# A hybrid recurrent decoder layer: ScalarE makes the convolution's first product from PSUM and the scaled diagonal of branch D, in place of GpSimd

## The chip, the core and the metric

The kernel runs on one core of one Trainium2 chip: TensorE for matrix products, VectorE, ScalarE and GpSimd for the rest, SyncE as the queue of the DMAs. The metric is the device time of one execution in microseconds, smaller is better. Each engine works through its own queue in order and waits on semaphores for the others. TensorE writes to PSUM; VectorE and ScalarE can read PSUM, GpSimd works on SBUF here.

## The reference

One inference step of one layer: layer norm, an input projection of 1024 to 3340 columns, four branches, an output projection, and a second layer norm. 2048 prompt tokens with 16 meta tokens ahead of them, and 8 sample sequences of 4 tokens, go through it.

```python
def _causal_conv(x, buf, w, b):          # branches A and C: 4 taps per channel, with bias
    xx = jnp.concatenate([buf, x], axis=1)
    y = lax.conv_general_dilated(xx, w[:, None, :], (1,), 'VALID', ..., feature_group_count=c)
    return y + b, xx[:, -3:]
...
xbc = jax.nn.silu(_causal_conv(xbc, ...))                  # A: Mamba-2 SSD
qkv = jax.nn.silu(_causal_conv(qkv, ...))                  # C: gated DeltaNet, q and k L2-normalised
...
def step(s, inp):                                          # D: HGRN2, per chunk
    qi, ki, vi, gi = inp                                   # gi: cumulated log decays
    dec = jnp.exp(jnp.where(i >= j, gi[:, :, None] - gi[:, None], -jnp.inf))
    a = jnp.einsum('bihk,bjhk,bijhk->bijh', qi, ki, dec)   # score matrix
    o = jnp.einsum('bijh,bjhv->bihv', a, vi) + jnp.einsum('bihk,bhkv->bihv', qi * jnp.exp(gi), s)
```

Branch B is a diagonal complex state space model (S5). All branch outputs are normalised per head or gated, concatenated, and projected back.

## The kernel before

All tensors are float32; products of the projections are made of high and low parts, three matrix products for each of 8 blocks of the 1024 input channels, so 24 for one block of results. The tokens are taken in two halves (`BLK`): half 0 in blocks of 304, 384 and 384 tokens, half 1 in two blocks of 512. For each half, phase 1a normalises and transposes the input, and phase 1b (`proj`) goes through column tiles of 128 channels; ten of these are convolution tiles (`conv_tile`: q, k and v of branch C, x, B and C of branch A). After both halves come the chunks of branches C and A, the gates, and the output projection.

TensorE runs in the order in which the program is written out. Chains that depend on each other ("jobs", such as `d_group` for branch D, `l2n`, `c_pre`, `b_main`) are generators that yield an estimate in microseconds; they are woven between the products of the projections by the sum of TensorE's costs so far. The order of most instructions on the other engines and of the DMAs on SyncE is set when the program is built, by a simulated timeline. The estimates in the yields stay the same in the change.

A projection's 24 products of a block go to a PSUM tile `pj`, of which there are two; when the block is done, `use` consumes it. In a convolution tile, `use` copies the block to `raw` (line 635, ScalarE; in the first block of half 0, where histories of the samples lie between the tokens, lines 626 to 632), with the last three columns of the block before in front of it. GpSimd then makes the product with the fourth tap and the bias into `cv` (line 639), VectorE adds the other three taps (line 641), and ScalarE takes the SiLU (lines 647 to 652). `raw` has three buffers, `cv` two. There are 50 such blocks: ten tiles by five blocks.

Branch D (`d_group`) takes two chunks of 128 tokens at a time (chunk 0 with 48 tokens alone): nine groups. The score matrix `AT` (128 x 8 x 128: token j, chunk and head, token i) starts as a diagonal, made from the column sums `sd` of q*k (line 1604, VectorE) and the identity by one wide product on GpSimd (line 1606). Then come levels s = 1, 2, 4 ... 64. In a level below 32, TensorE multiplies keys and queries, VectorE extends the queries `Q` (line 1666), GpSimd the keys `kS` (line 1667), and a predicated copy on VectorE (line 1670) puts the level's products into `AT`. The next level's products need lines 1666 and 1667 of this one. Line 580 makes the low parts of the next column tile's weights on GpSimd after ScalarE's rounding (line 579). Lines 1142 and 1151 are GpSimd's steps of branch B, lines 787 and 789 VectorE's steps of a triangular inverse.

Of the kernel before, what the change touches and what calls it, by code (L numbers as in the profile page):

```python
# [70 lines left out]
class Pinned:  # L71
    """An engine whose instructions don't move ahead of earlier ones."""
# [8 lines left out]
class Chain:  # L81
    """An engine whose instructions issued through here stay in the order in which they are written."""
# [14 lines left out]
class Kern:  # L97
# [12 lines left out]
    # The tensor engine runs in the order in which the kernel is written out. Dependent chains  # L110
    # are generators ("jobs") that yield the time until their next step can start; they are
    # woven between the matrix products of the projections.
# [64 lines left out]
    # ---------------------------------------------------------------- constants  # L177
    def consts(self, cp):
        nc, V, S, G = self.nc, self.V, self.S, self.G
        a = self.a  # L180
        self.ident = cp.tile([128, 128], F32, name="ident")
        make_identity(nc, self.ident)
        self.ones = cp.tile([128, 128], F32, name="ones")
        V.memset(self.ones, 1.0)
        self.triu = cp.tile([128, 128], F32, name="triu")
        G.affine_select(out=self.triu, in_=self.ones, compare_op=ALU.is_ge, fill=0.0,
                        base=0, pattern=[[1, 128]], channel_multiplier=-1)
        self.negm = cp.tile([128, 128], F32, name="negm")
        V.tensor_scalar(self.negm, self.triu, -1.0, 1e30, op0=ADD, op1=MUL)
        self.hsel = cp.tile([128, 2], F32, name="hsel")  # L190
        V.memset(self.hsel, 0.0)
        V.memset(self.hsel[0:64, 0:1], 1.0)
        V.memset(self.hsel[64:128, 1:2], 1.0)
        # sums the two parts of 32 channels of a head
        self.sel32 = cp.tile([128, 2, 32], F32, name="sel32")
        iv = self.ident.rearrange("p (a i) -> p a i", a=4)
        for h in range(2):
            V.tensor_tensor(self.sel32[:, h], iv[:, 2 * h], iv[:, 2 * h + 1], ADD)
        e9 = self.cst.rearrange("p a b -> p (a b)")[:NSEG, 0:48]
        V.memset(e9, 1.0)  # L200
        G.affine_select(out=e9, in_=e9, compare_op=ALU.is_ge, fill=0.0,
                        base=-12, pattern=[[1, 48]], channel_multiplier=-4)
        G.affine_select(out=e9, in_=e9, compare_op=ALU.is_ge, fill=0.0,
                        base=15, pattern=[[-1, 48]], channel_multiplier=4)
        V.memset(e9[0:1, 0:16], 1.0)
        p = self.pt()
        self.mm(p[:48, 0:48], e9, e9)
        self.segones = cp.tile([48, 48], F32, name="segones")
        V.tensor_copy(self.segones, p[:48, 0:48])
        p = self.pt()  # L210
        self.tr(p[:48, 0:NSEG], e9)
        self.segmask = cp.tile([48, NSEG], F32, name="segmask")
        V.tensor_copy(self.segmask, p[:48, 0:NSEG])
        self.triu_t = cp.tile([48, 48], F32, name="triu_t")
        V.tensor_tensor(self.triu_t, self.triu[:48, :48], self.segones, MUL)
        self.negm_t = cp.tile([48, 48], F32, name="negm_t")
        V.tensor_scalar(self.negm_t, self.triu_t, -1.0, 1e30, op0=ADD, op1=MUL)

    # ---------------------------------------------------------------- phase 1
    def small_loads(self, cp):  # L220
        """Job: small parameters, and the conv histories of the sample sequences channel-major."""
        a, V = self.a, self.Vp
        yield 8.2
        # channel-major small parameters, through one transpose
# [29 lines left out]
        # HGRN2 lower bound: softmax over the single layer, cumulative sum minus the first entry  # L254
# [70 lines left out]
    def phase1a(self, half, xp):  # L325
        """Layer norm and transposition of the input, and the products whose results are wanted token-major.
        The first yield comes before anything that needs the space of xh, xl or the weight ring."""
# [46 lines left out]
        def weights(i, parts):  # L374
            """u | i, dt, a, b: high and low parts."""
# [23 lines left out]
        else:  # L399
            # the first tile waits for as little as possible: one row comes by DMA, the other through the tensor engine  # L400
# [81 lines left out]
    def gates_in(self, half, sp):  # L482
# [3 lines left out]
        o = 1 - half          # chunk 0, the tail, is the first of half 0  # L486
# [14 lines left out]
        # softplus = max(x, 0) + log1p(e), log1p(e) = 2 atanh(e / (2 + e))  # L501
# [20 lines left out]
        # beta = sigmoid  # L522
# [7 lines left out]
        # inclusive cumulative sums inside each chunk, and the chunk totals  # L530
# [20 lines left out]
        if o:  # L551
            # decays of the tail segments, on every partition
# [8 lines left out]
        # rows: 0-7 cumulative logs, 8-15 their exponentials  # L561
# [21 lines left out]
    def proj(self, tiles):  # L583
        """tiles: (first column, per-block consumer, hook at the start); the next tile's weights are made ready first."""
# [20 lines left out]
    def conv_tile(self, i, c0, dst=None, nrm=None):  # L605
        """Causal conv and SiLU of one 128-channel tile, block by block.
        The first block is laid out as 8 x (3 history, 4 sample) | 3 zeros | meta | prompt."""
# [14 lines left out]
        def use(t0, n, p):  # L622
# [16 lines left out]
            G.tensor_scalar(cv[:, 0:m], raw[:, 3:3 + m], w[3], b, op0=MUL, op1=ADD)  # L639
# [22 lines left out]
    def l2n(self, st, dst, scale, nd, need, key):  # L662
        """Job: L2 normalisation over the channels of a head, for the blocks of a conv tile."""
# [54 lines left out]
    def decay(self, pool, tag, t, rows0, nh, bufs=None):  # L718
        """exp(acum_i - acum_j) for i >= j of one segment, 0 elsewhere, as [j, head, i]."""
# [10 lines left out]
    def c_pre(self, p):  # L730
        """Job: decayed K K^T and Q K^T of two heads, transposed."""
# [29 lines left out]
    def base_inv(self):  # L761
        """Inverses of the diagonal blocks of I + M, one block to a partition: 32 x 32 in the
        prompt chunks, 16 x 16 in chunk 0, whose segments don't cross multiples of 16."""
# [34 lines left out]
    def stream_out(self, c0, outs, mark=None):  # L798
        """outs: list of (function of (dst, psum)), dram destination)."""
# [53 lines left out]
    def conv_states(self):  # L853
        """Job: the conv states that go out."""
# [11 lines left out]
    # ---------------------------------------------------------------- branch B  # L866
    def exp_acc(self, pool, dst, x):
        """dst = exp(x) in float32 accuracy, for small tiles."""
# [20 lines left out]
    def b_setup(self, bp, tp):  # L889
# [56 lines left out]
        # powers of lambda, d = 0..8  # L946
# [21 lines left out]
        # rotating frame over chunks of 8  # L968
# [38 lines left out]
        # input matrices  # L1007
# [28 lines left out]
        # output matrices: Xc = (Cr | -Ci), Yc = (-Ci | -Cr)  # L1036
# [25 lines left out]
        # W1 = in-state matrices [(j q), (re n | im n)]  # L1062
# [15 lines left out]
        # block Toeplitz  # L1078
# [17 lines left out]
        # signed multipliers for single steps: h' = re * h + im_s * swap(h)  # L1096
# [187 lines left out]
    # ---------------------------------------------------------------- chunks  # L1284
# [85 lines left out]
    def c_inv(self, t0):  # L1370
        """Of two chunks: the inverse of I + M from the inverses of its 32 x 32 diagonal blocks,
        transposed; the values and the keys decayed to the end of the chunk, token-major."""
# [71 lines left out]
    def c_chunk(self, t, ep, y6):  # L1444
# [10 lines left out]
        # v_new = beta T (v - e^gc k S)  # L1455
# [33 lines left out]
    def c_head(self, ep, y6):  # L1489
        """Chunk 0: its nine segments start from their own states."""  # L1490
# [11 lines left out]
        # decay-scaled queries and keys  # L1502
# [50 lines left out]
    def tail_state(self, S9, kd, vflat, cdf, stage):  # L1553
        """S9[(h d), seg, pair, cols] <- decay * S9 + k^T v over each segment's tokens."""
# [21 lines left out]
    def d_group(self, t0c, nch, sfx):  # L1576
        """HGRN2 for nch chunks of 128 tokens (or chunk 0, 48 tokens); yields between its levels."""
# [22 lines left out]
        for c in range(nch):  # L1600
            for g in range(2):
# [4 lines left out]
        G.tensor_tensor(AT[:n, :4 * nch, :n], self.ident[:n, None, :n].to_broadcast([n, 4 * nch, n]),  # L1606
                        sd[:n, :nch].rearrange("p c h -> p (c h)")[:, :, None].to_broadcast([n, 4 * nch, n]), MUL)
# [6 lines left out]
        while s < lim:  # L1614
            # in the tail, blocks beyond 4 exist only in the 16 prompt tokens
# [9 lines left out]
            if s >= 32:  # L1625
                # few blocks: the keys block-diagonal by head, of the left halves alone
# [35 lines left out]
            # extend prefixes of the right halves, suffixes of the left halves, and the block products  # L1662
# [76 lines left out]
    def rms(self, t):  # L1739
        """Per-head RMS norms of a chunk."""  # L1740
# [5 lines left out]
        # The vector engine's transposes bring 32 channels at a time into the free dimension; small  # L1746
        # products add the two parts of a head and put the tokens onto their partitions.
# [28 lines left out]
    def gate(self, t):  # L1776
        """The norms and gates go onto a chunk."""
# [14 lines left out]
    def mix_chunk(self, t):  # L1792
        """The gated mix of a chunk, channel-major, rows A C D B, as high and low parts."""
# [11 lines left out]
    def out_setup(self, op, op2):  # L1805
        """Job: the output weights as high and low parts."""
# [19 lines left out]
    def out_chunk(self, t):  # L1826
# [24 lines left out]
        if last:  # L1851
            # the vector engine takes one part of the columns, the scalar engine and GpSimd the other
# [43 lines left out]
    def right_jobs(self):  # L1896
        """Branches B and D, in the space that phase 1 leaves, as their inputs come."""
# [66 lines left out]
    # ---------------------------------------------------------------- all  # L1964
# [89 lines left out]
    def head(self, ct):  # L2054
        """Chunk 0 of branches C and A."""
# [94 lines left out]
```

## Time and profile before

| | us |
|---|---|
| median of 3 runs | 1452.7 |
| lowest and highest run | 1446.28, 1456.98 |
| the profiled execution, first to last instruction (its span) | 1448.2 |
| TensorE busy (its weight loads) | 1294.9 (1090.3) |
| VectorE busy | 934.2 |
| GpSimd busy | 616.3 |
| ScalarE busy | 536.1 |

Of the profiled execution its own time is known as the span alone. How to read the rows: times are microseconds from the span's start unless marked ns; an engine is named PE (TensorE), PEld (its weight loads), DVE (VectorE), ACT (ScalarE), POOL (GpSimd), SP (SyncE). L639 is line 639 of the kernel. `out<-in` names tiles. In the timeline the brackets hold how long the engine had idled before the instruction and what it waited for. Busy time of VectorE and GpSimd includes time in which an instruction that has started stands still. PEclk is the granted TensorE clock: 1.00 is 2.4 GHz, 0.50 is 1.2 GHz.

### The profile page before, as it was taken

Reading aid. Unit: us, or ns where it says so; the run is one execution under the profiler, and the core shown is the slowest. Engines: PE = TensorE matmul, PEld = TensorE weight load, DVE = VectorE, ACT = ScalarE, POOL = GpSimd, SP = SyncE. Lnnn points to the kernel's source line nnn. Section 1 sums busy time; section 2 is a strip of 40 time slices with the busy share of each in tenths; the row PEclk is TensorE's granted clock in tenths of the full one; section 3 lists DMA queues with packets and bytes.
Section 4 is the critical chain, followed back from the end, with each engine's and each line's share of the span. In section 5 each row is a group of like instructions: output and inputs, shape, how many; then the busy total and the mean of one; then the engine's idle time right before and its main releaser. Section 6 shows DMA issues by size and latency. Waiting matters only on the chain. (4 is left out here: it accounts for less than half of the span.)

```text
span 1448.2 us, 23800 instructions
## 1 busy us (share of the span) xinstructions
PE 1294.9 (89%) x8596; PEld 1090.3 (75%) x8596; DVE 934.2 (65%) x2173; ACT 536.1 (37%) x1010; POOL 616.3 (43%) x508
## 2 busy tenths in 40 slices
PE   7984898899898999998996888789997999999997
PEld 6974788878877999877674677677775677777776
DVE  8899524557978549474355789962345676665654
ACT  3224256545214342353543442242434332333211
POOL 4065322524433312152434443441324476676665
PEclk9997999999989999999998899899998899999999
DMA  8511552464337434215534633125649777676333
GB/s 211 192 49 36 127 143 57 140 189 114 106 97 203 145 104 153 77 39 158 157 87 121 201 102 95 44 88 145 177 124 251 196 198 190 198 182 184 111 105 113
DMA packets 259007, 195.79 MB, mean 135 GB/s; under 512 B 70950, under 2 KB 231928, under 8 KB 258873
## 3 DMA queue, kind: packets, MB, share of 16 engines
q1 hardware_dynamic: 258890, 194.28, 47.2%
q8 instruction: 68, 1.11, 0.3%
q14 instruction: 49, 0.39, 0.1%
HBM read 125.01 MB, written 64.31 MB: 131 GB/s over the span
## 5 line engine op out<-in xcount | busy, mean ns | idle before, releaser
L126 PE MATMUL pj<-xh,w 128*128 128x384 f32 (+2 forms) x1760 | 547.8, 379 | 10.8 <-ACT raw L635 5.5
L126 PEld LDWEIGHTS pj<-xh,w 128*128 128x128 f32 x1760 | 339.7, 200 | 57.4 <-issue 11.6
L126 PE MATMUL pj<-xl,w 128*128 128x384 f32 (+2 forms) x880 | 322.8, 367 | 0.0
L126 PEld LDWEIGHTS pj<-xl,w 128*128 128x128 f32 x880 | 176.3, 200 | 12.4 <-issue 0.5
L580 POOL TENSOR_TENSOR w<-wr,w 128x1024 fp32r<-128x1024 f32 x44 | 109.9, 2497 | 85.6 <-ACT w L579 68.0
L641 DVE SCALAR_TENSOR_TENSOR cv<-raw,par,cv 128x384 f32<-128x384 f32 (+2 forms) x150 | 130.5, 872 | 9.5 <-POOL cv L639 8.2
L126 PE MATMUL pj<-woh,o_mh 128*128 128x512 f32 (+2 forms) x280 | 116.6, 416 | 6.3 <-DVE xt L1846 3.2
L126 PE MATMUL pj<-wol,o_mh 128*128 128x512 f32 (+2 forms) x280 | 109.4, 391 | 6.2 <-POOL wol L1817 5.9
L126 PE MATMUL pj<-woh,o_ml 128*128 128x512 f32 (+2 forms) x280 | 109.4, 391 | 0.0
L126 PE MATMUL pj<-w,xh 128*128 128x256 f32 (+3 forms) x544 | 105.2, 295 | 0.0
L639 POOL TENSOR_SCALAR cv<-raw,par 128x384 f32<-128x384 f32 (+2 forms) x50 | 49.3, 986 | 119.0 <-ACT raw L635 95.4
L126 PEld LDWEIGHTS pj<-w,xh 128*128 128x128 f32 (+1 forms) x544 | 84.6, 189 | 1.2 <-ACT xh L88 0.8
L126 PE MATMUL pj<-w,xl 128*128 128x256 f32 (+3 forms) x272 | 78.0, 291 | 0.8 <-DVE xl L88 0.8
L725 POOL TENSOR_TENSOR cdec<-cdec,negm 128x256 f32<-128x256 f32 x32 | 29.4, 921 | 98.6 <-DMA cdec<-rows_d 63.1
L126 PEld LDWEIGHTS pj<-woh,o_mh 128*128 128x128 f32 (+1 forms) x280 | 52.3, 187 | 18.6 <-DVE xt L1846 4.0
L126 PEld LDWEIGHTS pj<-wol,o_mh 128*128 128x128 f32 (+1 forms) x280 | 52.5, 188 | 16.0 <-POOL wol L1817 6.9
L1789 DVE TENSOR_TENSOR y<-y,f_R 128x768 f32<-128x768 f32 (+1 forms) x17 | 27.1, 1591 | 56.0 <-POOL f_R L1788 50.9
L126 PEld LDWEIGHTS pj<-woh,o_ml 128*128 128x128 f32 (+1 forms) x280 | 52.2, 187 | 12.3 <-issue 0.7
L308 POOL TENSOR_TENSOR lnrs<-lnve,mhalf 128x1 f32<-128x1 f32 (+1 forms) x34 | 24.5, 720 | 74.0 <-DVE lnve L88 46.2
L813 ACT ACTIVATE zs<-pj 128x384 f32<-128x384 f32 (+2 forms) x40 | 20.8, 520 | 87.6 <-PE pj L126 72.8
L126 PEld LDWEIGHTS pj<-w,xl 128*128 128x128 f32 (+1 forms) x272 | 51.2, 190 | 1.5 <-DVE xl L88 1.3
L1788 POOL TENSOR_TENSOR f_R<-f_R,f_z 128x768 f32<-128x768 f32 (+1 forms) x17 | 30.2, 1778 | 51.1 <-DMA f_R<-r_d 32.5
(570 smaller groups left out, 2687.8 us busy)
## 6 DMA issues: line engine op xcount, KB each, us to landing
wr<-in_w_in_dram SPq DMA_DIRECT2D x46, 512.0 KB
xt<-in_x_prompt_dram SPq DMA_DIRECT2D x16, 512.0 KB
xn_d<-xt SPq DMA_DIRECT2D x16, 512.0 KB
ma<-cma SPq DMA_DIRECT2D x64, 128.0 KB
xt<-xn_d SPq DMA_DIRECT2D x16, 512.0 KB
out_dram<-xt SPq DMA_DIRECT2D x15, 512.0 KB
f_R<-r_d SPq DMA_DIRECT2D x32, 192.0 KB
cdec<-rows_d SPq DMA_DIRECT2D x32, 128.0 KB
```

The source lines that it names most:

```text
L126: self._pe(self.PE.matmul(out, lhsT, rhs, start=start, stop=stop, **kw), 0.01 + n * (1 if rhs.dtype == F32R else 4) / 2400)
L308: self.G.tensor_tensor(rs[:n], ve[:n], self.mhalf[:n, 0:1], ALU.pow)
L580: self.G.tensor_tensor(w[:, :, 1], raw, w[:, :, 0].bitcast(F32), SUB)
L639: G.tensor_scalar(cv[:, 0:m], raw[:, 3:3 + m], w[3], b, op0=MUL, op1=ADD)
L641: V.scalar_tensor_tensor(cv[:, 0:m], raw[:, k:k + m], w[k], cv[:, 0:m], op0=MUL, op1=ADD)
L725: G.tensor_tensor(d[:n, :, :n], d[:n, :, :n], m[:n, None, :n].to_broadcast([n, nh, n]), ADD)
L813: S.activation(z, p, AF.Silu)
L1788: G.tensor_tensor(R[:, :, :n], R[:, :, :n], z[:, :, :n], MUL)
L1789: V.tensor_tensor(y6[:, 0:6, :n], y6[:, 0:6, :n], R[:, :, :n], MUL)
```

## The change

In the convolution, the product with the fourth tap and the bias is made by ScalarE directly from the projection's PSUM tile, except in the first block of half 0, where GpSimd makes it from `raw` as before. `raw` is still copied, since VectorE's other taps read it. In branch D, the wide product on GpSimd becomes 4 x `nch` activations on ScalarE (a copy scaled by a column of `sd`), one for each chunk and head, from the identity. That is 40 of the 50 products of line 639, and all nine of line 1606 (eight become eight activations each, the ninth becomes four). The rest of the diff removes comments.

```diff
             cv = self.rp.tile([128, 512], F32, name="cv", bufs=2)
-            G.tensor_scalar(cv[:, 0:m], raw[:, 3:3 + m], w[3], b, op0=MUL, op1=ADD)
+
+            if t0 == 0:
+                G.tensor_scalar(cv[:, 0:m], raw[:, 3:3 + m], w[3], b, op0=MUL, op1=ADD)
+            else:
+                S.activation(cv[:, 0:n], p[:, 0:n], AF.Identity, scale=w[3], bias=b)
             for k in range(3):
                 V.scalar_tensor_tensor(cv[:, 0:m], raw[:, k:k + m], w[k], cv[:, 0:m], op0=MUL, op1=ADD)
...
         AT = tp.tile([128, 8, 128], F32, name="d_AT" + sfx)
-        G.tensor_tensor(AT[:n, :4 * nch, :n], self.ident[:n, None, :n].to_broadcast([n, 4 * nch, n]),
-                        sd[:n, :nch].rearrange("p c h -> p (c h)")[:, :, None].to_broadcast([n, 4 * nch, n]), MUL)
+        for c in range(nch):
+            for h in range(4):
+                S.activation(AT[:n, 4 * c + h, :n], self.ident[:n, :n], AF.Copy, scale=sd[:n, c, h:h + 1])
```

## Rows read from the trace of the kernel before

**Rows 1.** Busy time by stretch: sum of 80-160, 360-470, 800-980; then the last 469.
```profile
sum 370.00, PE 305.09 PEld 262.65 DVE 315.59 ACT 128.87 POOL 167.74; mean PE 101.70 PEld 87.55 DVE 105.20 ACT 42.96 POOL 55.91
...
980.00:1449.00 469.00, 438.15 (x3287) 339.40 (x3286) 256.32 (x570) 148.21 (x269) 251.89 (x199) 0.95 0.61 167
```

**Rows 2.** Waits of TensorE, whole span: us in total, times, longest us.
```profile
PE pq L126 <- DVE Qa L1666: 16.7, 10, 6.4
...
PE pq L126 <- DVE b L1152: 12.2, 2, 9.2
...
PE pj L126 <- ACT raw L635: 5.5, 2, 3.1
...
PE pq L126 <- DVE Qb L1666: 5.1, 3, 2.6
```

**Rows 3.** Timeline at 438: VectorE, GpSimd, TensorE. Start us, us, instruction, idle before.
```profile
437.73 0.20 DVE L789 TENSOR_TENSOR acc<-acc,cdec 12x48 f32<-12x48 f32 x1
...
438.25 1.90 DVE L789 TENSOR_TENSOR acc<-acc,cdec 12x39 f32<-12x39 f32 x1
...
441.06 0.84 DVE L1666 TENSOR_TENSOR Qa<-Qa,d_qfa 64x256 f32<-64x256 f32 x2
...
442.23 1.28 DVE L1670 COPY_PREDICATED d_ATa<-lm,pq 128x512 f32<-128x512 uint8 x1
...
438.20 1.90 POOL L1606 TENSOR_TENSOR d_ATa<-ident,d_sda 128x1024 f32<-128x1024 f32 x1 [7.17 <-DVE d_sda L1604]
...
442.06 1.21 PE L126 MATMUL pq<-Qa,d_ka 128*128 128x128 f32 x7 [3.61 <-DVE Qa L1666]
```

**Rows 4.** Timeline at 902: VectorE, GpSimd.
```profile
902.31 2.38 DVE L641 SCALAR_TENSOR_TENSOR cv<-raw,par,cv 128x512 f32<-128x512 f32 x1
...
907.51 0.75 DVE L641 SCALAR_TENSOR_TENSOR cv<-raw,par,cv 128x512 f32<-128x512 f32 x1
...
902.10 2.05 POOL L1606 TENSOR_TENSOR d_ATa<-ident,d_sda 128x1024 f32<-128x1024 f32 x1 [1.05 <-DVE raw L634]
```

**Rows 5.** Timeline at 926: VectorE.
```profile
926.50 2.56 DVE L1666 TENSOR_TENSOR Qb<-Qb,d_qfb 64x256 f32<-64x256 f32 x2
```

**Rows 6.** GpSimd's busy time on line 639, then line 1606: the stretches of rows 1 summed.
```profile
sum 370.00, POOL 29.44; mean POOL 9.81
...
sum 370.00, POOL 10.57; mean POOL 3.52
```

**Rows 7.** Timeline at 1279, ScalarE: four activations in a row.
```profile
1279.19 1.28 ACT L727 ACTIVATE a_L<-a_L,nac 128x128 f32<-128x128 f32 x4 [0.35 <-POOL a_L L725]
```

**Rows 8.** Timeline at 827: VectorE, TensorE.
```profile
826.69 1.92 DVE L641 SCALAR_TENSOR_TENSOR cv<-raw,par,cv 128x512 f32<-128x512 f32 x1
...
831.09 1.29 PE L126 MATMUL pq<-acc 64*128 64x128 f32 x8 [1.37 <-DVE cma L753]
```

**Rows 9.** Groups by line and shape: count, busy us, mean ns, idle before and releasers.
```profile
L639 POOL TENSOR_SCALAR cv<-raw,par 128x512 f32<-128x512 f32 x20 | 20.1, 1003 | 57.3 <-ACT raw L635 57.3
...
L1194 ACT ACTIVATE b<-pq,par 128x512 f32<-128x512 f32 x8 | 5.5, 686 | 14.8 <-PE pq L126 11.5 <-DVE b L1195 3.3
...
L827 ACT ACTIVATE zs<-zs,lb,lb 128x512 f32<-128x512 f32 x4 | 3.3, 819 | 0.0
```

**Rows 10.** Timeline at 758, GpSimd.
```profile
758.30 3.31 POOL L639 TENSOR_SCALAR cv<-raw,par 128x512 f32<-128x512 f32 x1 [1.75 <-ACT raw L635]
761.58 2.82 POOL L580 TENSOR_TENSOR w<-wr,w 128x1024 fp32r<-128x1024 f32 x1
```

**Rows 11.** Waits of VectorE, whole span: us in total, times, longest us.
```profile
DVE cv L641 <- POOL cv L639: 8.2, 12, 2.2
```

**Rows 12.** Busy time by stretch (columns: PE, PEld, DVE, ACT, POOL, PEclk, DMA share, GB/s).
```profile
903.60:913.80 10.20, 6.17 (x19) 5.24 (x20) 10.02 (x17) 0.63 (x1) 3.91 (x4) 0.50 0.07 27
```

**Rows 13.** Timeline at 114 to 125: GpSimd, ScalarE.
```profile
123.40 0.66 POOL L639 TENSOR_SCALAR cv<-raw,par 128x384 f32<-128x384 f32 x1 [9.20 <-PE pq L120]
...
122.77 0.53 ACT L652 ACTIVATE acc<-cv 128x384 f32<-128x384 f32 x1
```

**Rows 14.** The page's costliest group: count, busy us, mean ns, idle before.
```profile
L126 PE MATMUL pj<-xh,w 128*128 128x384 f32 (+2 forms) x1760 | 547.8, 379 | 10.8 <-ACT raw L635 5.5
```

## The prediction

> **What bounds the kernel now.** I read four views. First the table of busy time by stretch, to see which engine has no slack and where. In the three stretches where the convolutions and branch D's first levels are dense (80 to 160, 360 to 470 and 800 to 980 us, 370 us together) TensorE is busy for 305.1 us, VectorE for 315.6, GpSimd for 167.7 and ScalarE for 128.9 [rows 1]. Those 370 us hold 65 us in which TensorE stands. The last 469 us, after the projections, have no instruction of the edited lines; there TensorE is busy for 438.2 of 469 [rows 1]. The matrix products run in the order in which they are written out, so the end moves by what happens to TensorE's idle time, and by its clock; work taken off another engine counts only where TensorE waits for it.
>
> Second, TensorE's waits: who ends its idle time. Ten waits, 16.7 us, end on line 1666 for tile Qa and three, 5.1 us, for Qb: VectorE's update of branch D's queries, which the products of the next level read. Two waits, 5.5 us, end on line 635, the copy that frees a bank of projection results [rows 2]. GpSimd's convolution product (line 639) and its diagonal (line 1606) do not end a wait of TensorE in these rows; they reach it only through VectorE.
>
> Third, the timeline around three of those waits shows how. At 438.20 GpSimd starts the diagonal and holds it for 1.90 us. VectorE's subtraction of a 12x39 tile at 438.25 takes 1.90 us, where the one before takes 0.20. Line 1666 can start at 441.06 only, and TensorE idles 3.61 us [rows 3]. At 902.10 GpSimd starts the next one that I follow, and a convolution step beside it takes 2.38 us, where the one of 907.51 takes 0.75 [rows 4]; the longest wait on Qa, 6.4 us, ends there [rows 2]. At 926.50 the pair of line 1666 takes 2.56 us [rows 5], where the pair of 441.06 takes 0.84 [rows 3]; the longest wait on Qb, 2.6 us, ends there [rows 2]. So while GpSimd runs this wide product, VectorE stands.
>
> Fourth, ScalarE's groups by shape, for the price of the new instructions.
>
> **Part 1, the diagonal.** Removed: nine products on GpSimd, 1.90 to 2.05 us each where rows stand [rows 3, 4]. Six of the nine lie in the three stretches with 10.6 us together [rows 6]. Added: eight ScalarE activations of 128x128 with a scale from a column in eight groups, four of 48x48 in the ninth. Four like ones (an exponential with a bias from a column) take 1.28 us back to back [rows 7], so eight take 2.56 and all nine groups 8 x 2.56 + 1.28 = 21.8 us of ScalarE. The diagonal is wanted by line 1670, the predicated copy. In the group at 438 it starts at 442.23, 4.0 us after GpSimd began the diagonal [rows 3]. ScalarE needs 2.56 us for it, so it is in time if ScalarE is free; without the stall line 1666 ends some 1.7 us earlier, and line 1670 would come 2.3 us after the diagonal's start and wait 0.2 us. If it isn't, line 1670 waits on VectorE, and behind it stands line 1666 of the next level, for which TensorE waits.
>
> What TensorE gains: the VectorE time lost behind the diagonal where TensorE was standing. At 438: 1.90 - 0.20 = 1.7 us. At 902: 2.38 - 0.75 = 1.6, and GpSimd's update of the keys (line 1667), which is queued behind the diagonal, comes 2 us earlier; I take 1.9. At 926: 2.56 - 0.84 = 1.7. At 826.7 a convolution step takes 1.92 instead of 0.75, so 1.2, and TensorE idles 1.37 at 831 [rows 8]. Together 6.5 us. In the other groups I count nothing: TensorE has projection products to run meanwhile, and no wait follows. The bounds: nothing, since line 1667 moves up into the freed place and can hold VectorE in its turn, and 10.6 us, all diagonals of the three stretches. I take 6.5, because the four waits are read one by one.
>
> **Part 2, the convolution's first product.** Removed: 40 of the 50 products on GpSimd, about 1.00 us each in the wide form [rows 9], 40 us in all; the ten first blocks of half 0 stay. Added: 40 activations from PSUM with scale and bias from columns. No row shows this form. Below it is a sigmoid from PSUM with one column, 686 ns for 128x512; above it is the identity with two columns from SBUF, 819 ns [rows 9]. I take 0.75 us, 30 us in all at most, since half of the blocks are narrower. The chain of a block is hardly shorter: before, a copy, then GpSimd's product; now the copy, then ScalarE's product. What goes is the time that GpSimd spends in it when something holds it there, 3.31 us at 758.30, and the wait of the work queued behind it, here line 580 at 761.58 [rows 10], inside the chain of branch B that lets TensorE idle for 9.2 us [rows 2].
>
> VectorE waited 8.2 us for line 639 in all [rows 11], in part for the ten blocks that stay. I take a gain of 4 us. The bounds: nothing, and 24 us: the 29.4 us that line 639 takes in the three stretches [rows 6], of which 40 in 50, if every one of them now holds up VectorE and TensorE behind it.
>
> **Part 3, ScalarE's load.** It rises by 21.8 + 30 = 52 us to about 588 us of 1448. The bank of a projection block is now freed by a second reader, 0.75 us after the first. TensorE has two such banks and runs 24 products into the other one meanwhile, so this is hidden behind them unless ScalarE is late. No DMA is issued by either moved step. The first of a group's activations waits for VectorE's column; queued behind it on ScalarE are the copies of line 635, for which TensorE waits. ScalarE was late with a bank twice, for 5.5 us [rows 2]: 2 x 0.75 = 1.5 us more, and I add 0.8 for a diagonal that gets ahead of a copy: 2.3 us. The bounds: nothing, and 40 x 0.75 = 30 us, each block waiting.
>
> **Part 4, the clock.** After the wait of 6.4 us the granted clock is 0.50, the lower level of 1.2 GHz, from 903.6 to 913.8, with TensorE busy for 6.17 of 10.2 us [rows 12]. At half clock those 6.17 us hold work for 3.1. Shorter waits may spare some of that; I take 2 us, with bounds of nothing and three times 3.1 = 9.
>
> **The sum.** -6.5 - 4 + 2.3 - 2 = -10.2 us on the span of 1448.2, so 1438.0. The median of the runs is 1452.7, 4.5 above that span, and the three runs lie between 1446.3 and 1457.0; by the same difference the forecast is 1442.5, rounded 1442.
>
> **The rivals.** *More gain, by the lock.* VectorE is busy for 315.6 of 370 us, 85%, in the stretches [rows 1], and the traces show it standing for all of a diagonal [rows 3, 5]. If each removed GpSimd product in the stretches held up VectorE, 24 + 10.6 = 34.6 us go, 85% of them from VectorE's queue: 29 us, and the time is 1423. For it: the three timelines. Against it: 65 us of TensorE's idle time in the stretches have other last causes too, and a convolution product is only 1.00 us long and often starts when VectorE waits for that very product. The Trainium skill, page SBUF — State Buffer, section "SBUF: two separate sides", states the rule that would make it so: GpSimd and a VectorE operation with two SBUF inputs share a port pair that one of them holds for its whole instruction, while ScalarE has ports of its own. By that rule the time would be this rival's 1423; rows 3 agree for the diagonal (1.90 us against 0.20), and no row read here shows it for line 639. Chance 0.17.
>
> *No change.* Line 1667, line 580 and the rest of GpSimd move up into the gaps and hold VectorE there instead, and the stalls of the three stretches end on VectorE's own amount of work. For it: line 1667 stands right behind the diagonal in the queue. Then the gain is 2 to 3 us, ScalarE takes it back, and the time is 1453. Chance 0.20.
>
> *Slower, by the ring of cv.* The bank is now freed by a product whose target has two buffers, and a buffer is free only after the SiLU of two blocks before. At 123.40 GpSimd's product had idled for 9.20 us; the SiLU before it ran at 122.77 and lasted 0.53, so it started when that buffer came free [rows 13]. On GpSimd this cost nobody a bank. On ScalarE the bank waits for it. A projection block keeps TensorE for about 9 us (24 products of 0.38 [rows 14]), so it costs something once VectorE is more than about one block late. If a third of the 40 blocks were late by 1.5 us the loss is 20 us, less 2 of gain: 1471. Against it: a second bank, and the copies before were already queued behind those SiLUs on ScalarE. Chance 0.12.
>
> **How the numbers follow.** The forecast has 0.51, with its own range of 1434 to 1450; 1442 is its middle. The own range holds the bounds of parts 1 and 2 as far as one of them comes out alone, and what a new order on ScalarE, GpSimd and SyncE may shift, since that order is simulated anew for the changed program. This kernel's measurement can tell about 1% from no change, so the limits are 1438 and 1467. Faster by over 1%: the first rival's 0.17 and 0.18 of the forecast's own lower part, 0.35. Slower: most of the last rival, 0.10. The rest, 0.55, lies within. To hold 8 in 10, the range takes the forecast and the no-change case whole and reaches towards both others: 1426 to 1460.
>
> **What would show it.** Right: line 1666 no longer takes over 1 us beside a GpSimd product at the first level of a group; TensorE's waits on Qa and Qb [rows 2] fall from 21.8 us to about 15; VectorE's total falls by 10 to 20 us; the edited product takes 0.7 to 0.8 us. Wrong: waits of TensorE on line 635 or on the new product above 10 us; line 1670 waiting for ScalarE; other GpSimd lines beside the same long VectorE instructions; or a gain in the last 469 us, which nothing here explains.

## The result: slower by 0.7%, with the predicted gains inside

| | kernel before | changed kernel |
|---|---|---|
| median of 20 runs, us | 1449.91 | 1460.58 |
| lowest and highest run, us | 1441.66, 1456.98 | 1452.49, 1468.53 |
| ratio, 95% interval | 1 | 1.0068 [1.005, 1.0085] |
| span of the profiled execution, us | 1448.2 | 1450.7 |

A second set of runs of the same changed program gave 1.0051 [1.0015, 1.0086]. The forecast was a fall of 0.7%; the time rose by 0.7%, just beyond the upper end of the range. The profiled execution of the changed kernel is the fastest of its 20 runs, so the two spans stand closer than the medians; what follows compares places in the traces, not the spans.

The changed kernel's page, its busy time by engine (lines of it answer to the table of before):

```profile
PE 1294.9 (89%) x8596; PEld 1090.1 (75%) x8596; DVE 909.8 (63%) x2173; ACT 583.4 (40%) x1120; POOL 566.9 (39%) x459
```

VectorE lost 24.4 us of busy time, GpSimd lost 49.4, ScalarE gained 47.3, TensorE has what it had. Busy time by stretch of the changed kernel, the three dense stretches summed and the last 469 us (columns of the second line: PE, PEld, DVE, ACT, POOL, PEclk, DMA share, GB/s):

```profile
sum 370.00, PE 310.67 PEld 265.11 DVE 308.32 ACT 157.06 POOL 134.82; mean PE 103.56 PEld 88.37 DVE 102.77 ACT 52.35 POOL 44.94
...
980.00:1449.00 469.00, 440.83 (x3285) 340.73 (x3283) 254.40 (x570) 148.27 (x269) 252.57 (x199) 0.95 0.61 167
```

Against [rows 1] VectorE is down by 7.3 us there and GpSimd by 32.9. The new instructions of the changed kernel, by form (count, busy us, mean ns, idle before):

```profile
L643 ACT ACTIVATE cv<-pj,par 128x512 f32<-128x512 f32 x20 | 15.6, 781 | 0.1
L1612 ACT ACTIVATE d_ATa<-ident,d_sda 128x128 f32<-128x128 f32 x48 | 14.7, 389 | 12.5 <-DVE d_sda L1608 12.5
L643 ACT ACTIVATE cv<-pj,par 128x384 f32<-128x384 f32 x20 | 13.5, 677 | 0.0
```

The product takes 0.78 us in the wide form and 0.68 in the narrow one; 0.75 was priced. All diagonals together take 20.6 us; 21.8 was priced. TensorE's waits in the changed kernel, whole span (us in total, times, longest):

```profile
PE pq L126 <- DVE b L1156: 16.0, 3, 8.0
PE pq L126 <- DVE g_g L521: 15.5, 1, 15.5
PE pq L126 <- DVE Qa L1671: 14.4, 10, 3.2
...
PE pq L126 <- DVE c_vb L1465: 5.2, 3, 3.9
...
PE pq L120 <- POOL l2r L699: 4.5, 1, 4.5
...
PE pq L126 <- DVE Qb L1671: 2.5, 4, 1.4
```

Qa and Qb (line 1671 is 1666 of before) fell from 21.8 us to 16.9 [rows 2], and the longest Qa wait from 6.4 to 3.2. (A further wait of 2.9 us that the view puts on line 1671 is left out: it belongs to a transposition of g_rw, which before waits 2.2 us there for ScalarE.) So the relief that the prediction looked for is there. Other waits stand higher than before: b, 12.2 there [rows 2], and these two:

```profile
PE pq L120 <- POOL l2r L695: 3.1, 1, 3.1
...
PE pq L126 <- DVE c_vb L1461: 0.4, 1, 0.4
```

The wait on g_g at 115 us is 8 us longer than before, but it costs nothing in the end: the lag of TensorE behind the kernel before is 7.5 us at 118 and gone by 140.

One price was missed in kind. Changed kernel, timeline at 448, VectorE, GpSimd, ScalarE:

```profile
447.99 1.97 DVE L1671 TENSOR_TENSOR Qa<-Qa,d_qfa 64x256 f32<-64x256 f32 x2
450.59 1.33 DVE L1675 COPY_PREDICATED d_ATa<-lm,pq 128x512 f32<-128x512 uint8 x1 [0.62 <-ACT d_ATa L1612]
...
448.00 0.88 POOL L795 COPY acc<-acc 12x256 f32<-12x256 f32 x1 [5.65 <-DVE acc L793]
...
448.11 2.45 ACT L1612 ACTIVATE d_ATa<-ident,d_sda 128x128 f32<-128x128 f32 x8 [0.39 <-DVE d_sda L1608]
```

The diagonal is off GpSimd, but line 795 has come into its place: it starts with VectorE's pair, and the pair takes 1.97 us where the undisturbed one took 0.84 [rows 3]. That is the "no change" rival at work in one group. The copy of line 1675 waits 0.62 us for ScalarE, where I had 0.2; over the whole run it waits so three times, 1.1 us.

### The profile page after: what moved, and what is told of

Its sections match the earlier page's. It is cut to its first block, busy times and chain, and to the rows that moved or that the text cites. A ratio compares the mean times of both kernels' runs of the same rounds, so it can differ in the third digit from the quotient of the medians.

```text
span 1450.7 us, 23815 instructions
## 1 busy us (share of the span) xinstructions
PE 1294.9 (89%) x8596; PEld 1090.1 (75%) x8596; DVE 909.8 (63%) x2173; ACT 583.4 (40%) x1120; POOL 566.9 (39%) x459
## 4 chain that ended last, share of the span: by engine, by line
PE 30%; DVE 14%; DMA 10%; POOL 7%; issue 4%; ACT 4%; SPq 2%; POOLq 0%; DVEq 0%; ACTq 0%
PE pj L126 17%; PE pq L126 11%; DMA f_R<-r_d 2%; DVE cv L645 2%; DMA r_d<-f_rs 2%; PE pq L120 2%; POOL f_R L1793 1%; DVE cdec L791 1%; DMA c_q<-qkv_d 1%; DVE Qa L1671 1%; POOL xt L1870 1%; POOL xt L1871 1%; DMA cdec<-rows_d 1%; DVE y L1794 1%; DVE acc L793 1%
## 5 line engine op out<-in xcount | busy, mean ns | idle before, releaser
L645 DVE SCALAR_TENSOR_TENSOR cv<-raw,par,cv 128x512 f32<-128x512 f32 (+2 forms) x150 | 119.9, 800 | 9.2 <-ACT cv L643 4.7
L308 POOL TENSOR_TENSOR lnrs<-lnve,mhalf 128x1 f32<-128x1 f32 (+1 forms) x34 | 24.4, 719 | 79.8 <-DVE lnve L88 45.5
L579 ACT CAST w<-wr 128x1024 fp32r<-128x1024 f32 x44 | 45.9, 1043 | 16.7 <-PE pj L126 8.6
```

Source lines behind the costliest of these rows:

```text
L308: self.G.tensor_tensor(rs[:n], ve[:n], self.mhalf[:n, 0:1], ALU.pow)
L579: S.copy(w[:, :, 0], raw)
L645: V.scalar_tensor_tensor(cv[:, 0:m], raw[:, k:k + m], w[k], cv[:, 0:m], op0=MUL, op1=ADD)
```

## The experiments

All ratios are to the kernel before, timed beside it on the same chip, in five rounds. The planner below is the simulated timeline that sets the order of ScalarE, VectorE, GpSimd and SyncE when the program is built.

### Which edit, which half

conv_only is the changed kernel with the diagonal back on GpSimd (the lines of the change's diff taken back), diag_only the one with all products back on GpSimd, after_again the changed kernel itself. conv_half1_diag leaves half 0's products on GpSimd:

```diff
-            if t0 == 0:
+            if not half:
                 G.tensor_scalar(cv[:, 0:m], raw[:, 3:3 + m], w[3], b, op0=MUL, op1=ADD)
```

conv_only: 

> Only the 40 convolution products go to ScalarE; the diagonal stays on GpSimd. Theory A (the convolution's product on ScalarE is what costs, in half 0, where ScalarE's in-order queue and branch B's chains meet; the diagonal gains 5 to 7 us): 1.010 to 1.014 of before, with TensorE's waits on lines 1671 and 1670 still near 20 us. Theory B (the diagonal's 68 activations cost, by getting ahead of ScalarE's copies): 0.997 to 1.000. Theory C (neither step costs by itself; the order that is planned anew for all engines and DMAs moves the time): anything from 0.995 to 1.010, and the two parts alone do not add up to the change.

diag_only: 

> Only the diagonal goes to ScalarE; all 50 convolution products stay on GpSimd. Theory A: 0.993 to 0.997 of before, with TensorE's waits on the query update down from 21.8 us to about 15. Theory B: 1.006 to 1.010. Theory C: anything from 0.995 to 1.010, without the waits on the query update having to do with it.

conv_half1_diag: 

> The diagonal on ScalarE, and the convolution's product on ScalarE in half 1 alone (20 blocks); half 0 as before. The trace of the change loses 13 us between 160 and 340 us, in half 0, and gains in half 1. Theory A: 0.990 to 0.997. Theory B: 1.004 to 1.010. Theory C: no rule, 0.995 to 1.010.

after_again: 

> The changed kernel once more, for a second trace: 1.005 to 1.009 of before. If its loss is settled by the plan and the engines, the lag of TensorE behind the kernel before again builds up between 160 and 340 us (10 to 14 us) and is paid back by 940; if that stretch was chance in one execution, the lag lies elsewhere.

| run | ratio | 95% interval |
|---|---|---|
| conv_only | 1.0109 | 1.0064 to 1.0155 |
| diag_only | 0.998 | 0.9949 to 1.0012 |
| conv_half1_diag | 0.9936 | 0.9908 to 0.9964 |
| after_again | 1.0051 | 1.0015 to 1.0086 |

conv_only and conv_half1_diag lie in the ranges of theory A, diag_only just above its range, with the waits on the query update at 14.9 us as that theory had it. The lag that after_again was to show between 160 and 340 us is there in both traces of the changed kernel, 13 us in the first and 18 in the second; it was paid back by 940 us in the first alone, and 8 us were left in the second.

The loss seemed to sit in half 0's 20 products. From that came theory S: ScalarE's own added work delays the chains that TensorE waits for in half 0.

### Where in half 0

Four versions of conv_half1_diag. h0_kq0 moves k0 and q0 of half 0 to ScalarE too, h0_kq1 k1 and q1 (tiles 5 and 7), h0_vx the six others:

```diff
-            if not half:
+            if t0 == 0 or not (half or i in (4, 6)):
```

h0_double adds ScalarE's load ahead of half 0's product on GpSimd:

```diff
+                if t0:
+                    S.activation(p[:, 0:n], p[:, 0:n], AF.Identity, scale=w[3], bias=b)
```

h0_kq0: 

> Both changes on ScalarE in half 1 and in the groups, and in half 0 only for the first two convolution tiles (k0, q0: 4 of half 0's 20 products, at 94, 101, 114 and 132 us). Without those 4 the ratio was 0.9936; with all 20 it was 1.0051 to 1.0068, so the 20 cost 0.012. Theory S (the cost is ScalarE's own work and its in-order place, the same for every product): 4/20 of it, 0.996. Theory O (the cost is the new order in the stretch of the second k and q tiles, 238 to 300 us, with branch B beside it): none here, 0.991 to 0.996, and TensorE's lag against the kernel before, 7 us at 115, is gone by 135.

h0_kq1: 

> The same with only k1 and q1 of half 0 on ScalarE (4 of the 20 products, at 238, 245, 263 and 267 us). Theory S: 0.996. Theory O: most of the 0.012 is here, 1.000 to 1.005, with a wait of TensorE on the l2r of GpSimd (line 699) of about 4.5 us at 276 in place of 3.1 and a clock below 0.9 in 280:300.

h0_vx: 

> The same with only the v and x, B, C tiles of half 0 on ScalarE (12 of the 20 products, 337 to 440 us). Theory S: 12/20 of 0.012, 1.001. Theory O: about nothing, 0.991 to 0.997; if the half 0 stretch 360 to 470 gains as half 1 did, 0.990.

h0_double: 

> As the version at 0.9936 (half 1 and the diagonal on ScalarE), and in half 0 ScalarE makes the 20 products as well, in place in PSUM where nobody reads them, while GpSimd's product feeds the convolution as before: ScalarE's load and the later release of the PSUM bank without any relief of GpSimd. Theory S: all of the cost, 1.004 to 1.008. Theory O: little of it, 0.992 to 0.998.

Measured: 1.0006 [0.998, 1.0031], 0.9993 [0.9963, 1.0023], 1.0025 [0.9998, 1.0052] and 0.9984 [0.9955, 1.0013]. Over 0.9936 the three groups cost 0.007, 0.006 and 0.009, 0.022 together, where all 20 products at once cost 0.012 to 0.013. Four products cost nearly as much as twelve. The doubled load costs 0.005, less than half of what theory S wanted. Two traces show what theory O told of them, h0_kq1 a wait of 4.5 us on l2r, h0_kq0 a lag of 7.5 us at 115 that is gone by 135, but neither theory predicted the pattern of the times.

### Theory S falls

h0_none is conv_half1_diag without half 0's fourth tap:

```diff
+            if not half and t0:
+                V.tensor_scalar(cv[:, 0:m], raw[:, 0:m], w[0], b, op0=MUL, op1=ADD)
...
-            for k in range(3):
+            for k in range(1 if t0 and not half else 0, 3):
```

half1_both is conv_half1_diag with the diagonal on ScalarE only in half 1 (`t0c >= 9`), conv_half1 the one with all diagonals on GpSimd, half1_diag_again the same program once more.

half1_both: 

> Both edits in half 1 alone: half 0 is the kernel before, its four full groups of branch D and the short one included; in half 1 ScalarE makes the 20 convolution products and the four diagonals. Theory S/L (ScalarE's extra instructions lengthen the dependent chains of half 0, which TensorE waits for; half 1 has TensorE ahead and gains): 0.990 to 0.996, TensorE level with the kernel before up to 470 us. Rival (the 0.9936 of the version with the diagonal in both halves came from half 0's diagonals, or from a lucky set of runs): 0.997 to 1.001.

half1_diag_again: 

> The version at 0.9936 a second time, beside the others. If that was a steady property: 0.991 to 0.996. If it was luck of its set of runs, and every variant of half 0 in the second call (0.998 to 1.0025) is then less of a loss: 0.997 to 1.000.

h0_none: 

> The same with the fourth tap left out in half 0's 20 blocks (VectorE's first tap takes the bias, nobody makes the product): GpSimd is relieved and ScalarE gets nothing. If ScalarE's added work is the loss: no loss against the version above, 0.988 to 0.995. If the loss comes from what GpSimd's relief moves up (another order, another meeting of GpSimd and VectorE): 0.999 to 1.006.

conv_half1: 

> The convolution product on ScalarE in half 1 alone, the diagonal on GpSimd as before. The diagonal alone was 0.998. If the two add: 0.995 to 0.998. If the diagonal on ScalarE is worth more beside the convolution product there (the lock of lines 902 and 926 falls away only with both): 0.998 to 1.002.

| run | ratio | 95% interval |
|---|---|---|
| half1_both | 1.0028 | 1.0005 to 1.0052 |
| half1_diag_again | 0.9914 | 0.9881 to 0.9948 |
| h0_none | 1.0035 | 1.0004 to 1.0066 |
| conv_half1 | 1.0053 | 1.0025 to 1.008 |

half1_both and conv_half1 lie above every range expected for them; h0_none lies in the range for another order. The version at 0.9936 is repeatable. But leaving half 0's products out altogether, with nothing added to ScalarE there and a tap less for VectorE to add, costs 1% against it. So does taking half 0's diagonals back to GpSimd. The convolution in half 1 alone is 0.5% slower than before, and with the diagonals, which alone give 0.2%, it is 0.6 to 0.9% faster. No sum of fixed prices, one for each moved part, gives these numbers. What all variants share is that each is ordered anew: between the changed kernel and the kernel before, 602 of VectorE's 2173 instructions and 161 of the 1047 DMAs on SyncE stand in another place (counted in the two programs, the moved instructions aside).

### The order kept

The next six keep the order of a known kernel on all four queues by an edge (order only, no wait) from each instruction to its successor, and change the engine alone. A moved convolution product stands right behind its raw copy in ScalarE's queue.

```diff
         Kern(tc, a, o).run()
+        keep_order(tc, nc)
...
+def keep_order(tc, nc):
+    for part in _ORDER.split(";"):
...
+            if prev is not None:
+                tc.add_manual_dep(q[k], prev, mybir.DependencyInfo(
+                    mybir.DependencyClass.NoSync, mybir.DependencyReason.DATA), reason="order")
+            prev = q[k].name
```

conv_only_order: 

> The convolution's 40 products on ScalarE, the diagonal on GpSimd (1.0109 when the planner ordered the work anew), but with the order of the kernel before kept on ScalarE, VectorE, GpSimd and SyncE by an edge from each instruction to the next: each moved product comes right behind its raw copy in ScalarE's queue (two of them behind the SiLU that frees their buffer). Theory O (the loss is the new order that the planner gives, not the work on ScalarE): 0.993 to 1.000. Theory E (ScalarE's added products lengthen the chains): 1.007 to 1.013.

conv_half1_order: 

> The 20 products of half 1 on ScalarE (1.0053 when ordered anew), in the kept order of the kernel before; half 0 is then the kernel before instruction by instruction. Theory O: 0.994 to 1.000. Theory E: 1.003 to 1.007.

after_order: 

> The whole change (1.0051 to 1.0068), in the kept order of the version with half 0's products on GpSimd (0.9914 to 0.9936): only half 0's 20 products stand in another queue. Theory O: 0.989 to 0.996. Theory E: 1.003 to 1.008.

after_border: 

> The whole change in the kept order of the kernel before; the diagonals' copies stand in ScalarE's queue where GpSimd's product stood in time. Theory O, and the lock of GpSimd's diagonal on VectorE falls away: 0.988 to 0.997, the waits on lines 1671 at 10 us or less. Theory E: 1.003 to 1.008.

before_aorder: 

> The other corner: GpSimd makes all products and diagonals, as before, in the kept order of the changed kernel (each of GpSimd's moved instructions stands in its queue where ScalarE's stood in time). If order and engine add, by 1.0068 and 1.0051 for both and 0.993 for the engine alone: the order alone is 1.012 to 1.014, so 1.008 to 1.017. If the order is bad only together with ScalarE's work: 0.997 to 1.005.

diag_order: 

> The diagonal alone on ScalarE in the kept order of the kernel before (0.998 when ordered anew). The convolution alone was 0.999 in that order and both were 0.993. If the two add: 0.991 to 0.996. If the gain needs both (GpSimd's products still meet VectorE): 0.997 to 1.001.

| engines of | order of | ratio | 95% interval | same engines, ordered anew |
|---|---|---|---|---|
| conv_only | before | 0.999 | 0.9955 to 1.0026 | 1.0109 |
| conv_half1 | before | 0.9993 | 0.996 to 1.0026 | 1.0053 |
| diag_only | before | 0.9949 | 0.9924 to 0.9975 | 0.998 |
| changed kernel | before | 0.993 | 0.9896 to 0.9963 | 1.0051, 1.0068 |
| changed kernel | conv_half1_diag | 0.9935 | 0.9897 to 0.9972 | 1.0051, 1.0068 |
| before | changed kernel | 1.0242 | 1.021 to 1.0273 | 1 |

That settles where the loss lies: the same engines' work gains in one order and loses in the other. In the kept order the change is faster by 0.7%, and now the parts add within the noise: 0.1% for the convolution and 0.5% for the diagonal against 0.7% for both. The order was kept on the chip too: in the trace of after_border SyncE's 1047 DMAs follow each other as in the kernel before, by their tiles, and VectorE's instructions all but 3. What was not run is the changed kernel with its own order kept by edges, which would show by itself that the edges cost and give nothing; conv_half1_order, whose half 0 is the kernel before with edges, is at 0.9993. The new order costs the changed kernel 1.2 to 1.4% (1.0051 or 1.0068 by 0.993), 18 to 20 us. Given to the engines of before it costs 2.4%, more than the 0.8 to 1.7% expected: there GpSimd's products stand in places that were found for ScalarE's, which may cost something besides; that was not tried apart.

TensorE's waits on Qa and Qb, expected at 10 us or less for the changed kernel in the order of before, are 15.3. With the diagonal alone in that order (diag_order) they are 15.8, for 21.8 before:

```profile
PE pq L126 <- DVE Qa L1671: 13.3, 10, 4.7
...
PE pq L126 <- DVE Qb L1671: 2.5, 3, 1.4
```

### One place where the new order loses

TensorE's order is the same in all these programs, so the end of one and the same matrix product can be compared between two traces. From 260 to 300 us (branch B beside the tiles k1 and q1) the changed kernel falls 4.8 us further behind the kernel before; in the kept order it gains 0.3 us there. Busy time in that stretch of the kernel before, the changed kernel and the changed kernel in the order of before (PEclk is the third number from the end):

```profile
260.00:300.00 40.00, 35.74 (x275) 31.52 (x274) 21.96 (x35) 21.93 (x36) 16.56 (x7) 0.96 0.59 168
```
```profile
260.00:300.00 40.00, 32.92 (x249) 31.54 (x249) 18.92 (x29) 21.69 (x35) 18.32 (x6) 0.87 0.47 132
```
```profile
260.00:300.00 40.00, 34.72 (x274) 30.85 (x273) 21.26 (x32) 22.68 (x37) 16.40 (x6) 1.00 0.60 164
```

249 products against 275 and 274, and a granted clock of 0.87 against 0.96 and 1.00. In the changed kernel TensorE stands twice in this stretch, both times ahead of a transposition of l2r, the reciprocal norms of `l2n`. The two waits there, then the same two in the kernel before:

```profile
276.72 0.39 PE L120 MATMUL pq<-ident,l2r 128*18 128x128 f32 x1 [4.49 <-POOL l2r L699]
...
294.48 0.27 PE L120 MATMUL pq<-ident,l2r 128*18 128x128 f32 x1 [2.59 <-DVE b L1144]
```
```profile
269.18 0.39 PE L120 MATMUL pq<-ident,l2r 128*18 128x128 f32 x1 [3.10 <-POOL l2r L695]
...
285.07 0.27 PE L120 MATMUL pq<-ident,l2r 128*18 128x128 f32 x1 [1.16 <-DVE b L1140]
```

Around each wait of the changed kernel the granted clock is at its lower level (same columns):

```profile
274.20:281.00 6.80, 4.28 (x14) 4.28 (x15) 3.66 (x7) 1.99 (x3) 4.87 (x2) 0.50 0.83 204
...
294.70:298.10 3.40, 3.40 (x13) 3.40 (x12) 0.28 (x1) 2.58 (x5) 0.00 (x0) 0.50 0.43 139
```

In the kernel before it is there once, from 268.7 to 272.1, and in the kept order not at all. VectorE, GpSimd and SyncE of the changed kernel:

```profile
271.25 0.16 DVE L698 TENSOR_SCALAR l2r<-pq 128x18 f32<-128x18 f32 x1
271.33 2.31 DVE L1149 TENSOR_TENSOR_SCAN b<-rdec,b 128x1040 f32<-128x1040 f32 x1
273.56 0.58 DVE L645 SCALAR_TENSOR_TENSOR cv<-raw,par,cv 128x384 f32<-128x384 f32 x1
274.08 0.54 DVE L687 TENSOR_REDUCE l2p<-sq 128x12 f32<-128x384 f32 x1
...
289.39 0.72 DVE L717 TENSOR_TENSOR acc<-acc,bc 128x536 f32<-128x536 f32 x1 [7.21 <-DMA bc<-nrm]
...
271.49 5.18 POOL L699 TENSOR_TENSOR l2r<-l2r,mhalf 128x18 f32<-128x18 f32 x1 [0.58 <-DVE l2r L698]
...
276.98 0.41 SPq L578 DMA_DIRECT2D wr<-in_w_in_dram  x1
278.21 0.37 SPq L1191 DMA_DIRECT2D b<-z_d  x1
278.64 0.38 SPq L707 DMA_DIRECT2D nrm<-l2s  x1
284.05 0.63 SPq L712 DMA_DIRECT2D bc<-nrm  x1
```

The same of the changed kernel in the order of before:

```profile
268.30 0.17 DVE L698 TENSOR_SCALAR l2r<-pq 128x18 f32<-128x18 f32 x1
268.39 0.54 DVE L687 TENSOR_REDUCE l2p<-sq 128x12 f32<-128x384 f32 x1
268.85 2.31 DVE L1149 TENSOR_TENSOR_SCAN b<-rdec,b 128x1040 f32<-128x1040 f32 x1
...
282.89 1.34 DVE L717 TENSOR_TENSOR acc<-acc,bc 128x536 f32<-128x536 f32 x2 [3.19 <-DMA bc<-nrm]
...
268.55 3.23 POOL L699 TENSOR_TENSOR l2r<-l2r,mhalf 128x18 f32<-128x18 f32 x1 [0.58 <-DVE l2r L698]
...
267.99 0.38 SPq L578 DMA_DIRECT2D wr<-in_w_in_dram  x1
...
274.70 0.30 SPq L707 DMA_DIRECT2D nrm<-l2s  x1
275.63 0.37 SPq L1191 DMA_DIRECT2D b<-z_d  x1
276.70 0.64 SPq L712 DMA_DIRECT2D bc<-nrm  x1
```

Instructions have changed places on two engines. VectorE takes its scan (line 1149) ahead of a reduction of 0.54 us (line 687), and GpSimd's power of 18 columns (line 699), for which TensorE waits, takes 5.18 us instead of 3.23. SyncE issues the 512 KB of the next weights (line 578) 1.66 us before the small store of the norms (line 707) instead of 6.71 us before it, and another load of 512 KB (line 1191, branch B) 0.4 us before the store instead of 0.9 us behind it. The loads that read the norms back go out 5.41 us after the store instead of 2.00; VectorE's scaling by them (line 717) starts at 289.39 instead of 282.89. By the Trainium skill, page DMA: Bandwidth & Descriptors, section "Queues, rings and completion order", a queue's descriptors are taken in ring order on each DMA engine, and a completion lands only after that engine's earlier writes; a store behind two large loads would then have to wait for them, and these rows agree with that.

All traces fall into two groups here (the lag is the growth from 260 to 300 us, worked out from the ends of the same product in each trace and that of before):

| | weights to store, us | load of line 1191 to store, us | store to reload, us | line 699, us | lag, us |
|---|---|---|---|---|---|
| changed kernel, after_again, conv_only, h0_kq1, h0_none, h0_double, before_aorder | 1.60 to 1.66 | 0.42 | 5.14 to 5.41 | 5.17 to 5.18 | 4.6 to 5.3 |
| the kernel before and the twelve others, all but one of those in a kept order among them | 6.71 to 6.72 | 0.9 behind it | 1.98 to 2.00 | 3.23 | -0.3 to 1.3 |

In half 0's convolution h0_none puts no work on ScalarE and h0_double takes none off GpSimd; both are in the first group. So 5 us of the 18 to 20 are placed, as an effect of the order. Both changes carry them, each through one of TensorE's two waits: the first, which ends on line 699, is 1.4 us longer than before; the second, for the l2r that line 717's late start holds up, is also 1.4 us longer. The remaining 2 us go with the lower clock around the two waits, which holds for 10.2 us in the changed kernel and for 3.4 before. Why line 699 is longer, and which of the two loads holds the store, wasn't tried apart.

The rest of the loss is not placed. Between 160 and 340 us, 260 to 300 included, both traces of the changed kernel fall 13 and 18 us behind the kernel before, and the changed kernel falls 5.6 us behind in the order of before. Between 980 and 1260 us, with no edited instruction, TensorE waits on c_vb (line 1465, VectorE in branch C) for 5.2, 5.5, 4.0, 5.8 and 6.0 us in the changed kernel, after_again, conv_only, h0_none and conv_half1, which have the highest ratios but one, and for 0.4 in the kernel before and in after_border. But the lag doesn't follow this wait: from 980 to 1260 us it grows by 4.9 us in the changed kernel, by 6.9 in after_border, and by 13.6 in diag_only, where the wait is 0.4 too. The clock goes along with the loss: the mean granted clock over the runs is 0.928 for the changed kernel, 0.929 to 0.931 for before, 0.934 in the order of before and 0.921 for before_aorder, and between runs of one kernel 0.01 of clock goes with about 9 us (5 to 13 in the sets of ten runs and more).

## Why the prediction was wrong, by its own steps

**What bounds the kernel** held. TensorE's idle time and its clock decided; ScalarE's and GpSimd's loads did not.

**Part 1** was right in mechanism and size: 6.5 us forecast; the diagonal alone in the kept order gives 0.51% of 1455.6 us, 7.4 us (3.6 to 11.1). In that trace the waits on Qa and Qb fell by 6.0 us. Followed product by product, those at 442, 907 and 929 us of the kernel before, 3.6, 6.4 and 2.6 us, became 1.4, 4.7 and 0.9: 5.7 us less, where 5.3 were priced. The fourth wait, at 831, went, but its neighbours grew: 5.7 us together before, 6.1 after, so the 1.2 us priced there did not come. The bound below it, that other GpSimd work moves into the place, was real in the group at 448.

**Parts 2 and 3** together were -4 + 2.3 = -1.7 us; the convolution alone in the kept order gives -0.1%, -1.5 us (-6.6 to +3.8), which agrees but can't be told from zero. VectorE's waits for the product fell from 8.2 us [rows 11] to 5.4 in that trace, 3.3 of them for the products that stay on GpSimd and 2.1 for ScalarE's; 4 us were taken. TensorE's waits for a bank in the kept order are 7.5 us on line 643 with both edits, 2 us over the 5.5 of [rows 2]; 2.3 was priced.

**Part 4** had the right sign. In the kept order the granted clock is 0.91 between 900 and 940 us, where the kernel before had 0.84, and the mean over the runs is 0.934 against 0.930; its size can't be read apart from the waits.

**The sum** of -10.2 us is what the change gives in the kept order: 0.7% of 1457.3 us, 10.2 us, with an interval of 5 to 15. The agreement to a tenth is luck: the interval is that wide, and the terms hit it only in part.

**The step that failed** is in "How the numbers follow": "what a new order on ScalarE, GpSimd and SyncE may shift, since that order is simulated anew for the changed program" stood there as some width of the forecast's own range. It was no term and no rival, and it was 18 to 20 us, nearly twice the sum, and on the other side. I see no row of before that gives its sign. Runs of variants give its size: any of these programs is one draw of an order, and the draws measured here with about the same work lie between 0.991 and 1.011. Why the planner's order is worse is known for 5 us alone; for the rest the cause stays open.

**The rivals.** *More gain by the lock* (1423) was refuted: with all diagonals and 40 of 50 products off GpSimd and the order kept, 0.993 is all that comes. VectorE's busy time did fall by 24.6 us there, but no more than those 10 us reached the time. *Slower, by the ring of cv* did not decide: TensorE's waits on the new product are 3.7 us in the changed kernel and 7.5 in the kept order. A third buffer for cv was not tried. *No change* was half right, for the wrong reason: the gain was given back, in one group by a GpSimd instruction in the freed place, on the whole by the new order.

**What would show it**: of the signs of being right, the product at 0.68 to 0.78 us for 0.7 to 0.8 came as told, Qa and Qb at 16.9 us for about 15 nearly, and VectorE's total fell by more than told, 24.4 us for 10 to 20; line 1671 still took 1.97 us beside a GpSimd instruction at 448. Two signs of being wrong came too: another GpSimd line beside the same VectorE pair, and line 1675 waiting for ScalarE, 1.1 us in all. Neither is near the size of the loss; the list held marks of the mechanism and none that would have shown the order.

## What to carry to other kernels

Where a planner orders the queues anew for each program, an edit is timed together with a draw of a new order, and here the draw was worth 1 to 2%, the edit 0.7%. Time a local edit once in the kept order of the kernel before, and only then let the planner loose; forecast with a term for the order, of both signs and as wide as variants of the same work lie apart. Four versions here beat both kernels: the change with half 0's products left on GpSimd (0.9914 and 0.9936), the whole change in that version's order (0.9935) or in the order of before (0.993), and the diagonal alone in the order of before (0.9949).

## What the runs showed that I had not expected

Less work can cost time: with 20 products left out and VectorE's first tap cheaper, the kernel was 1% slower than with them. A small store that is issued 1.6 and 0.4 us after two loads of 512 KB was followed by its reload after 5.1 to 5.4 us in seven traces of seven, and after 2.0 us in the thirteen where one load was 6.7 us ahead and the other behind it. At this place a GpSimd power on 18 columns took 5.17 us in the seven traces in which VectorE's scan had started 0.15 us ahead of it, and 3.23 us in the thirteen in which the scan started 0.3 us after it; that the scan is the reason is not shown.
